# Front products of a decoder layer in 512 weight columns a matmul instead of 256

## The chip, the core and the metric

One core of a Trainium2 chip runs the whole layer. The engines in what follows are PE (TensorE, the matmuls), PEld (its weight loads), DVE (VectorE), ACT (ScalarE), POOL (GpSimd) and SP (SyncE, whose queue starts most of the transfers). The metric is device time in microseconds (us) for one execution, the median of several.

## What is computed

A decoder layer on 256 tokens of 1024 features, float32 throughout:

```python
h = layer_norm(DEEPNORM_ALPHA * h + hybrid_mixer(h, ...))        # DSA heads and GLA heads, then w_out
h = layer_norm(DEEPNORM_ALPHA * h + memory_cross_attention(h, mem, w_q, w_k, w_v, w_o))
h = layer_norm(DEEPNORM_ALPHA * h + peer(h, ...))                # product keys, 16 experts a head of 16384
# in hybrid_mixer: proj = x @ w_in, split in q, k, v, q_idx, k_idx, w_idx, g_q, g_k, g_v, g_lr, g_r
#   DSA: index scores pick 64 keys a query, softmax attention over those; GLA: gated linear attention
#   y = concat(y_dsa, y_gla) @ w_out
# in memory_cross_attention: k = mem @ w_k, v = mem @ w_v
```

The products that the change touches are `x @ w_in` for q, k, v, g_v and g_r, the mixer's output `y @ w_out`, and the first 512 of the 1024 columns of `mem @ w_v`.

## The kernel before

A float32 product is made of three float32r products: each operand is split in a rounded part and a remainder (`whi`, `wlo` for a weight; `xPh`, `xPl` for the input, likewise `yP`, `mP`, `hP`), and hi·hi, hi·lo and lo·hi are summed in PSUM.

Weights come in tiles of 1 MB, `w`, from a ring of three buffers; `wget` (L115) issues the transfer on SP's queue. `split` (L233) takes half a tile: ACT writes `whi` (L237), then DVE writes `wlo` (L239). Both lie in a ring `gd` of five buffers, so at most two and a half pairs exist at once, and a new `whi` or `wlo` waits until PE has finished with a pair. A half tile is 24 matmuls of 256 columns.

`proj` (L252) multiplies for both blocks of 128 tokens with the token block stationary and the weights moving. Its weight tile holds all 1024 rows of 256 columns; the two tiles of a 512-column result (`w1a`, `w1b` and so on) fill the two halves of one PSUM bank. `projT` (L268) does the transposed products (g_q, g_k, memory keys, queries) with the weights stationary and 256 token columns moving.

The front of the program is a set of generators, played in an order written out by hand: `FRONT` (L51) has a letter a step, `p` for the input products (q, k, gqk, v, gr, gv in that order), `a` and `b` for index selection and sparse attention of the two token blocks, `g` for linear attention, `m` for the memory keys and values. Then `MID` (L53) plays the mixer output (`mixed`, L828) against the rest of `m`. A scheduler then sets each engine's order from its own estimate of durations, so the order on an engine can differ from the text. Each engine works through its own order without overtaking.

The front's DVE work beside `wlo` is chiefly the index selection: `sc` (L394, L396) sums scores, and eight rounds of MAX (L402) and MATCH_REPLACE (L403) find the 64 largest. After the mixer output come layer norm 1 (L186 to L196), the queries (`mm<-hP`), memory attention, layer norm 2, and the expert part: row gathers on POOL (L899), the dense products `sc<-h2T,d` fed by transfers, and 1536 products `py` at the end.

Of the kernel before, what the change touches and what calls it, by code (L numbers as in the profile page):

```python
# [13 lines left out]
FT = mybir.dt.float32  # L14
# [4 lines left out]
AF = mybir.ActivationFunctionType  # L19
# [64 lines left out]
def kernel(ctx: ExitStack, tc, I, out):  # L84
    nc = tc.nc
    vec, act, gp = nc.vector, nc.scalar, nc.gpsimd
    pe = Counted(nc.tensor)
# [5 lines left out]
    wpool = ctxL.enter_context(tc.tile_pool(name="wpool", bufs=3))  # L93
# [6 lines left out]
    def mmt(name="mm"):  # L100
        return pmm.tile([128, 512], FT, tag="mm", name=name)
# [14 lines left out]
    def wget(nm):  # L116

        if nm in first:
            return first.pop(nm)
        src = I[nm]  # L120
        t = wpool.tile([128, 8, 256], FT, tag="w", name="w")
        nc.sync.dma_start(out=t[:, :, :src.shape[2]], in_=src)
        return t


# [5 lines left out]
    for i in range(4):  # L131
        k, cs = i // 2, slice(2 * (i % 2), 2 * (i % 2) + 2)
# [6 lines left out]
    ii = load(consts, "ii", [128, 2, 128])  # L139
    ident, iot = ii[:, 0, :], ii[:, 1, :]  # L140
    first["w1a"] = wget("w1a")
    gup = load(pers, "gup", [16, 256])
    gmask = load(pers, "gmask", [128, 128], I32)
# [6 lines left out]
    xv = pers.tile([128, 2, DM], FT, name="xv")  # L150
# [82 lines left out]
    def split(src, n, c=4):  # L233

        hi = gath.tile([128, c, n], FR, tag="gd", name="whi")
        lo = gath.tile([128, c, n], FR, tag="gd", name="wlo")
        act.activation(hi, src, AF.Copy)  # L237
        eng = gp if POOL[next(turn) % len(POOL)] else vec
        eng.tensor_sub(lo, src, hi.bitcast(FT))  # L239
        return hi, lo  # L240

    def pair(name):
        return [[slot(name + h, [128, 4, S], FR) for k in range(2)] for h in "hl"]

    def split_to(x, k, src, at=slice(None)):
        act.activation(x[0][k][at], src, AF.Copy)  # L246
        vec.tensor_sub(x[1][k][at], src, x[0][k][at].bitcast(FT))

    def parts(a, b):
        return ((a[0], b[0]), (a[0], b[1]), (a[1], b[0]))  # L250

    def proj(xP, nms, ps):  # L252

        o = 0
        for nm in nms:
            w = wget(nm)
            n = I[nm].shape[2]
            for k in range(2):
                wp = split(w[:, 4 * k:4 * k + 4, :n], n)
                for b in range(2):  # L260
                    for c in range(4):
                        for m, (l, r) in enumerate(parts([x[k] for x in xP], wp)):
                            pe.matmul(ps[b][:, o:o + n], lhsT=l[:, c, b * 128:(b + 1) * 128], rhs=r[:, c, :],
                                      start=(k == 0 and c == 0 and m == 0), stop=(k == 1 and c == 3 and m == 2))
                    yield
            o += n

    def projT(nm, xP, ps):  # L268

        w = wget(nm)  # L270
        for k in range(2):
            wp = split(w[:, 4 * k:4 * k + 4, :], 256)
            yield from products_T(wp[0], wp[1], xP, ps, k)
# [54 lines left out]
    def proj_in(nms, name, n):  # L328
        ps = [mmt() for _ in B2]
        yield from proj(xP, nms, ps)  # L330
        for b in B2:
            t = V[b][name]
            act.activation(t, ps[b][:, :n] if len(t.shape) == 2 else
                           ps[b][:, :n].rearrange("p (h d) -> p h d", d=t.shape[2]), AF.Copy)
# [237 lines left out]
    def memory_keys():  # L572
        memT = wget("memT")
        mP = pair("mP")
        for k in range(2):
            split_to(mP, k, memT[:, 4 * k:4 * k + 4])
        for i in range(4):
            ps = [mmt(), mmt()]
            yield from projT("xk%d" % i, mP, ps)
            for e in range(2):  # L580
                act.activation(xkT[:, 2 * i + e, :], ps[e][:, 0:256], AF.Copy)
        done.add("xk")
        for i in range(4):
            ps = [mmt(), mmt()]
            yield from proj(mP, ["xv%d" % i], ps)
            for m in range(2):
                act.activation(xv[:, m, i * 256:(i + 1) * 256], ps[m][:, 0:256], AF.Copy)

    def residual(b, xT_, nm, src, dst):

# [176 lines left out]
    xP = pair("xP")  # L767
# [45 lines left out]
    def play(streams, score):  # L813

        for ch in score:
            next(streams[ch], None)

    mk = memory_keys()
    front = dict(a=itertools.chain(index_select(0), sparse_attention(0)),
                 b=itertools.chain(index_select(1), sparse_attention(1)),  # L820
# [10 lines left out]
    def mixed():  # L831
        for i in range(2):
            nc.sync.dma_start(out=gb[:, i], in_=bcast_row(I["lnr"][i:i + 1, :], DM))
        for i in range(2):
            ps = [mmt() for _ in B2]
            yield from proj(yP, ["wo%d" % (2 * i), "wo%d" % (2 * i + 1)], ps)
            cs = slice(i * 512, (i + 1) * 512)
            for b in B2:
                vec.scalar_tensor_tensor(r1[b][:, cs], xb[b][:, cs], ALPHA, ps[b], op0=OP.mult, op1=OP.add)
        for b in B2:  # L840
            layer_norm(r1[b], (gb[:, 0], gb[:, 1]), h1[b], small)
# [219 lines left out]
    for now in range(128):  # L1061
        for i, span in enumerate(PICKS):
            if now >= span[0]:
                if i not in gpick:
                    begin(i)
                n = 18 if todo[i][2] == 2 else 12
# [10 lines left out]
        if now == CHANGE:  # L1077
            ctxP.close()
            wp = ctxB.enter_context(tc.tile_pool(name="wp", bufs=2))
# [100 lines left out]
    for b in B2:  # L1180
# [5 lines left out]
        if b == 0:  # L1186
# [4 lines left out]
            cs = slice(FB, DM)  # L1191
# [8 lines left out]
    cs = slice(0, FB)  # L1200
# [6 lines left out]
def _chunk(w, cols):  # L1207

    return np.ascontiguousarray(w[:, cols].reshape(8, 128, -1).transpose(1, 0, 2))
# [55 lines left out]
```

## Time and profile before

| what | before |
|---|---|
| median of 3 runs | 1048.31 us (1044.84 to 1048.84) |
| the profiled execution, device time | 1042.45 us |
| its span, first to last instruction | 1040.7 us |
| PE busy | 937.0 us (90%), 6650 matmuls |
| PEld busy | 870.2 us (84%) |
| DVE busy | 826.9 us (79%) |
| ACT busy | 420.2 us (40%) |
| POOL busy | 386.9 us (37%) |
| mean granted clock of PE | 0.966 of 2.4 GHz |

Shares over the whole span hide that the stages differ. A matmul's busy time overlaps the next one's, so what a product costs is read from start to start of a run of them, not from its own duration. Where an engine stands idle, the view says what released it; where it is not idle, its order alone sets the time.

### The profile page before, as it was taken

The numbers are of one execution on the slowest core, as the hardware profiler recorded it, in microseconds if no ns is written. First come the engines' busy times: TensorE is split into PE (matmuls) and PEld (weight loads), VectorE is DVE, ScalarE is ACT, GpSimd is POOL, SyncE is SP. The second block draws the span as 40 slices with busy tenths as digits, with TensorE's granted clock in tenths as the row PEclk, the third lists the DMA queues.
The fourth block names the chain that finished last, engine by engine and source line by source line (L and its number), as shares of the span: only waits on it lengthen the run. The fifth ranks groups of instructions, "written<-read, shape, count | busy, mean of one in ns | idle before, by whom it ended". The sixth has DMA issues, their size and how long they took to land.

```text
span 1040.7 us, 17837 instructions
## 1 busy us (share of the span) xinstructions
PE 937.0 (90%) x6650; PEld 870.2 (84%) x6650; DVE 826.9 (79%) x1944; ACT 420.2 (40%) x686; POOL 386.9 (37%) x263
## 2 busy tenths in 40 slices
PE   6999999897866977988699989899999999999994
PEld 6998879897756977887599989899888888888883
DVE  5967866745797998996699975855888988889896
ACT  5548664353211232322022231322655555655561
POOL 0000000000447454334545510000577777777772
PEclk9999999898998989999899989999999999999997
DMA  8555233445699989999989989264799999999992
GB/s 291 187 168 197 82 123 127 163 161 198 240 340 322 374 283 409 384 403 400 367 302 369 403 319 326 97 218 161 273 324 316 324 320 319 317 321 317 326 316 72
DMA packets 73974, 285.13 MB, mean 274 GB/s; under 512 B 9488, under 2 KB 10016, under 8 KB 67872
## 3 DMA queue, kind: packets, MB, share of 16 engines
q1 hardware_dynamic: 46976, 190.66, 51.5%
q0 software_dynamic: 26624, 92.29, 24.0%
q8 instruction: 52, 0.85, 0.3%
q10 hardware_dynamic: 288, 1.05, 0.3%
q14 instruction: 34, 0.28, 0.1%
HBM read 282.91 MB, written 1.05 MB: 273 GB/s over the span
## 4 chain that ended last, share of the span: by engine, by line
PE 62%; DVE 14%; DMA 14%; issue 4%; ACT 3%; POOL 1%; SPq 0%; ACTq 0%; POOLq 0%; DVEq 0%
PE py L76 28%; PE mm L76 17%; PE sc L76 10%; DMA d<-dnT 9%; DMA gd<-dn,ei 4%; DVE gd L901 4%; DVE oa L1008 3%; PE wb L76 3%; DVE o L1003 2%; POOL gd L899 1%; PE tp L80 1%; DVE wlo L239 1%; DMA w<-xo 1%; PE go L76 1%; ACT whi L237 1%
## 5 line engine op out<-in xcount | busy, mean ns | idle before, releaser
L899 POOL DMA_INDIRECT gd<-dn,ei x128 | 160.6, 1255 | 430.9 <-ACT s1b L877 268.3
L934 POOL DMA_INDIRECT gu<-upg,ei x128 | 221.6, 1731 | 203.2 <-DVE yq L1120 133.5
L76 PE MATMUL sc<-h2T,d 128*128 128x128 f32 x2048 | 255.0, 280 | 25.9 <-DMA d<-dnT 24.6
L76 PEld LDWEIGHTS sc<-h2T,d 128*128 128x128 f32 x2048 | 242.6, 195 | 32.9 <-DMA d<-dnT 16.2
L76 PE MATMUL py<-uh,w 128*128 128x320 f32 (+1 forms) x1024 | 235.5, 352 | 1.0 <-ACT uh L1153 1.0
L76 PEld LDWEIGHTS py<-uh,w 128*128 128x128 f32 x1024 | 177.4, 189 | 22.9 <-ACT uh L1153 1.2
L1153 ACT ACTIVATE uh<-u 128x1024 fp32r<-128x1024 f32 x128 | 135.7, 1062 | 116.9 <-PE py L76 77.6
L1154 DVE TENSOR_TENSOR ul<-u,uh 128x1024 fp32r<-128x1024 f32 x128 | 156.5, 1224 | 31.0 <-issue 16.1
L901 DVE CUSTOM_DVE_ANT_0 gd<-gd,h 128x1024 f32<-128x1024 f32 x128 | 155.2, 1224 | 23.8 <-DMA gd<-dn,ei 23.7
L76 PE MATMUL py<-ul,w 128*128 128x320 f32 (+1 forms) x512 | 138.9, 352 | 0.7 <-DVE ul L1154 0.7
L239 DVE TENSOR_TENSOR wlo<-w,whi 128x1024 fp32r<-128x1024 f32 (+1 forms) x68 | 81.3, 1197 | 47.5 <-PE mm L76 35.7
L76 PEld LDWEIGHTS py<-ul,w 128*128 128x128 f32 x512 | 91.1, 189 | 12.5 <-DVE ul L1154 1.0
L237 ACT ACTIVATE whi<-w 128x1024 fp32r<-128x1024 f32 (+1 forms) x68 | 70.4, 1038 | 54.1 <-PE mm L76 40.1
L1008 DVE TENSOR_SCALAR oa<-ii,ixT,wT 128x128 f32<-128x128 f32 x256 | 72.5, 359 | 23.3 <-PE wb L76 22.5
L76 PE MATMUL wb<-oa,o 128*128 128x128 f32 x512 | 75.1, 287 | 13.3 <-DVE oa L1008 13.2
L1012 ACT ACTIVATE W<-wb 128x512 f32<-128x512 f32 x64 | 38.2, 596 | 117.6 <-PE wb L76 114.1
L76 PEld LDWEIGHTS wb<-oa,o 128*128 128x128 f32 x512 | 66.7, 196 | 16.0 <-DVE oa L1008 9.2
L1122 DVE SCALAR_TENSOR_TENSOR yq<-gu,wt,yq 128x384 f32<-128x384 f32 x127 | 78.0, 614 | 0.1
L76 PE MATMUL mm<-h2T,w 128*128 128x128 f32 x448 | 54.9, 283 | 3.4 <-DMA w<-pq 3.4
L76 PEld LDWEIGHTS mm<-h2T,w 128*128 128x128 f32 x448 | 53.7, 200 | 4.1 <-DMA w<-pq 4.1
L76 PE MATMUL mm<-whi,xPh 128*128 128x256 f32 (+1 forms) x176 | 50.9, 292 | 6.6 <-ACT xPh L246 6.6
L76 PE MATMUL mm<-wlo,xPh 128*128 128x256 f32 (+1 forms) x176 | 52.0, 296 | 1.6 <-DVE wlo L239 1.6
(327 smaller groups left out, 1369.7 us busy)
## 6 DMA issues: line engine op xcount, KB each, us to landing
d<-dnT SPq DMA_DIRECT2D x128, 512.0 KB
u<-upd SPq DMA_DIRECT2D x128, 512.0 KB
w<-pq SPq DMA_DIRECT2D x10, 1024.0 KB
w<-xo SPq DMA_DIRECT2D x8, 1024.0 KB
w<-xk SPq DMA_DIRECT2D x4, 1024.0 KB
w<-xv SPq DMA_DIRECT2D x4, 1024.0 KB
w<-wo SPq DMA_DIRECT2D x4, 1024.0 KB
w<-xq SPq DMA_DIRECT2D x4, 1024.0 KB
```

The costliest lines, as they stand in the source:

```text
L76: self.eng.matmul(out, lhsT=lhsT, rhs=rhs, **kw)
L237: act.activation(hi, src, AF.Copy)
L239: eng.tensor_sub(lo, src, hi.bitcast(FT))
L899: gp.indirect_dma_start(out=g, out_offset=None, in_=I["dn"], in_offset=bass.IndirectOffsetOnAxis(ap=ei[:, k:k + 1], axis=0))
L901: vec.tensor_tensor_reduce(out=g, in0=g, in1=H2[0], scale=1.0, scalar=0.0, op0=OP.mult, op1=OP.add, accum_out=wt[:, k:k + 1])
L934: gp.indirect_dma_start(out=g, out_offset=None, in_=I["upg"], in_offset=bass.IndirectOffsetOnAxis(ap=PK[b]["ei"][:, k:k + 1], axis=0))
L1003: vec.tensor_tensor(o2, iot[:, None, :].to_broadcast([128, 8, 128]), ix2[:, 4 * g:4 * g + 8, None].to_broadcast([128, 8, 128]), op=OP.is_e ...
L1008: vec.tensor_scalar(a, iot, ixT[:, t:t + 1], wT[:, t:t + 1], op0=OP.is_equal, op1=OP.mult)
L1012: act.activation(W[0][:, :, 4 * g - 4:4 * g], ps[g - 1].rearrange("p (j i) -> p i j", j=4), AF.Copy)
L1122: vec.scalar_tensor_tensor(y, g, wt[:, k:k + 1], y, op0=OP.mult, op1=OP.add)
L1153: act.activation(uh, u, AF.Copy)
L1154: vec.tensor_sub(ul, u, uh.bitcast(FT))
```

## The change

The weights of q, k, v, g_v, g_r, of the mixer output and of the first half of the memory values are laid out so that a 1 MB tile holds 512 rows of 512 columns instead of 1024 rows of 256. `proj` now runs over two such tiles; a half tile is two chunks of 128 rows by 512 columns, still 1024 elements a partition for ACT and DVE, and 12 matmuls of 512 columns instead of 24 of 256. A matmul writes a whole PSUM bank. `proj_256` is the old form, kept for the last two memory value tiles, which come later. The number of steps a tile is played in stays four. Bytes, transfers and splits stay as many as before.

```diff
 def wget(nm):
-        t = wpool.tile([128, 8, 256], FT, tag="w", name="w")
-        nc.sync.dma_start(out=t[:, :, :src.shape[2]], in_=src)
+        t = wpool.tile([128, src.shape[1], src.shape[2]], FT, tag="w", name="w")
+        nc.sync.dma_start(out=t, in_=src)
...
     def proj(xP, nms, ps):
-        o = 0
-        for nm in nms:
+        for k, nm in enumerate(nms):
             w = wget(nm)
             n = I[nm].shape[2]
-            for k in range(2):
-                wp = split(w[:, 4 * k:4 * k + 4, :n], n)
+            for h in range(2):
+                wp = split(w[:, 2 * h:2 * h + 2, :], n, 2)
                 for b in range(2):
-                    for c in range(4):
-                        for m, (l, r) in enumerate(parts([x[k] for x in xP], wp)):
-                            pe.matmul(ps[b][:, o:o + n], lhsT=l[:, c, b * 128:(b + 1) * 128], rhs=r[:, c, :],
-                                      start=(k == 0 and c == 0 and m == 0), stop=(k == 1 and c == 3 and m == 2))
+                    for c in range(2):
+                        xs = [x[k][:, 2 * h + c, b * 128:(b + 1) * 128] for x in xP]
+                        for m, (l, r) in enumerate(parts(xs, wp)):
+                            pe.matmul(ps[b][:, 0:n], lhsT=l, rhs=r[:, c, :], start=(k == 0 and h == 0 and c == 0 and m == 0),
+                                      stop=(k == 1 and h == 1 and c == 1 and m == 2))
                     yield
-            o += n
...
-        for i in range(4):
+        for o, n in ((0, 512), (512, 256), (768, 256)):
             ps = [mmt(), mmt()]
-            yield from proj(mP, ["xv%d" % i], ps)
+            yield from proj(mP, ["xv0", "xv1"], ps) if n == 512 else proj_256(mP, "xv%d" % (o // 256), ps)
             for m in range(2):
-                act.activation(xv[:, m, i * 256:(i + 1) * 256], ps[m][:, 0:256], AF.Copy)
+                act.activation(xv[:, m, o:o + n], ps[m][:, 0:n], AF.Copy)
```

PE's order has 384 rows fewer than before, one for each pair of matmuls that became one. Lines from `projT` on move by 11 (L394 is L405). Beyond that the scheduler moves a few instructions of the front. On DVE, at the first index scores (`sc`; `wlo` here is the second half of the second q tile), before:

```order
L374 COPY glr<-tp 16x128
L394 TENSOR_SCALAR sc<-rl,wi 128x256
L396 SCALAR_TENSOR_TENSOR sc<-rl,wi,sc 128x256 x5
L239 TENSOR_TENSOR wlo<-w,whi 128x1024
L396 SCALAR_TENSOR_TENSOR sc<-rl,wi,sc 128x256 x2
L399 TENSOR_TENSOR sc<-sc,cst 128x128
```

and now:

```order
L385 COPY glr<-tp 16x128
L239 TENSOR_TENSOR wlo<-w,whi 128x1024
L405 TENSOR_SCALAR sc<-rl,wi 128x256
L407 SCALAR_TENSOR_TENSOR sc<-rl,wi,sc 128x256 x7
L410 TENSOR_TENSOR sc<-sc,cst 128x128
```

The remainder moved from the middle of the scores to ahead of them.

On ACT, in the first linear attention (`gl`, its gates) and where the memory keys begin (`whi` is the first half of their first tile), before:

```order
L475 ACTIVATE gl<-gl 128x256
L485 ACT_TABLE_LOAD
L485 ACTIVATE gl<-gl 128x256
L486 ACTIVATE gl<-gl 128x256
L237 ACTIVATE whi<-w 128x1024
```

and now:

```order
L486 ACTIVATE gl<-gl 128x256
L237 ACTIVATE whi<-w 128x1024
L496 ACT_TABLE_LOAD
L496 ACTIVATE gl<-gl 128x256
L497 ACTIVATE gl<-gl 128x256
```

The rounded part went ahead of the table load and two gate functions.

On PE, where the mixer output (`yP`) follows the memory values (`mP`) and the last transposes of linear attention (`yg`) stand, before:

```order
L76 MATMUL mm<-whi,mPl 128x256
L80 MATMUL tp<-ii,yg 128x128 x4
L76 MATMUL mm<-whi,mPh 128x256
L76 MATMUL mm<-wlo,mPh 128x256
L76 MATMUL mm<-whi,mPl 128x256
L76 MATMUL mm<-whi,yPh 128x256
```

and now:

```order
L76 MATMUL mm<-whi,yPh 128x512
L76 MATMUL mm<-wlo,yPh 128x512
L76 MATMUL mm<-whi,yPl 128x512
L76 MATMUL mm<-whi,yPh 128x512
L76 MATMUL mm<-wlo,yPh 128x512
L80 MATMUL tp<-ii,yg 128x128 x4
L76 MATMUL mm<-whi,yPl 128x512
```

The transposes moved from ahead of the last three memory products to behind the eighth matmul of the mixer output.

## Rows read from the trace of the kernel before

**Rows 1.** Busy time by stretch: length, PE, PEld, DVE, ACT, POOL; clock, DMA share, GB/s.
```profile
33.00:61.00 28.00, 27.77 (x234) 27.07 (x235) 27.05 (x81) 13.99 (x21) 0.00 (x0) 1.00 0.48 166
61.00:81.00 20.00, 20.00 (x168) 19.87 (x167) 8.85 (x10) 9.49 (x11) 0.00 (x0) 1.00 0.61 211
81.00:99.00 18.00, 16.86 (x139) 16.30 (x139) 14.81 (x21) 15.98 (x28) 0.00 (x0) 1.00 0.38 138
137.00:161.00 24.00, 23.05 (x178) 18.06 (x177) 17.16 (x49) 14.63 (x40) 0.00 (x0) 1.00 0.23 88
161.00:183.00 22.00, 22.00 (x186) 22.00 (x184) 13.06 (x13) 9.24 (x10) 0.00 (x0) 1.00 0.48 167
183.00:198.00 15.00, 10.88 (x78) 10.30 (x76) 14.65 (x39) 5.52 (x8) 0.00 (x0) 0.82 0.49 179
273.00:500.00 227.00, 181.58 (x1365) 168.84 (x1366) 197.51 (x720) 53.01 (x125) 107.82 (x89) 0.95 0.96 363
```

**Rows 2.** The chain that ended last: start us, length us, what.
```profile
33.20 11.95 PE mm L76 x95
...
60.72 18.88 PE mm L76 x155
...
273.64 7.97 DMA gd<-dn,ei
```

**Rows 3.** PE's instructions in order: start us, duration us; input products, 33 starts apart.
```profile
62.02 0.28 PE L76 MATMUL mm<-whi,xPl 128*128 128x256 f32 x1
...
65.98 0.28 PE L76 MATMUL mm<-whi,xPl 128*128 128x256 f32 x1
```

**Rows 4.** The same view in the last stage, `py`: pairs of 512 and of 320 columns.
```profile
757.22 0.62 PE L76 MATMUL py<-ul,w 128*128 128x512 f32 x2
757.68 0.91 PE L76 MATMUL py<-uh,w 128*128 128x512 f32 x4
758.43 0.46 PE L76 MATMUL py<-ul,w 128*128 128x320 f32 x2
758.72 0.92 PE L76 MATMUL py<-uh,w 128*128 128x320 f32 x4
```

**Rows 5.** The same view: the scores' matmuls, first remainder products of four half tiles.
```profile
23.76 1.17 PE L76 MATMUL dots<-kiT,qiT 32*128 32x256 f32 x16
...
29.84 0.39 PE L76 MATMUL mm<-wlo,xPh 128*128 128x256 f32 x1 [0.90 <-DVE wlo L239]
...
33.20 0.39 PE L76 MATMUL mm<-wlo,xPh 128*128 128x256 f32 x1 [0.23 <-DVE wlo L239]
...
39.16 0.39 PE L76 MATMUL mm<-wlo,xPh 128*128 128x256 f32 x1
...
42.14 0.39 PE L76 MATMUL mm<-wlo,xPh 128*128 128x256 f32 x1
```

**Rows 6.** DVE's instructions in order, the index scores and first selection rounds.
```profile
25.55 0.35 DVE L394 TENSOR_SCALAR sc<-rl,wi 128x256 f32<-128x256 f32 x1 [2.28 <-ACT rl L389]
...
28.57 1.22 DVE L239 TENSOR_TENSOR wlo<-w,whi 128x1024 fp32r<-128x1024 f32 x1
29.71 1.00 DVE L396 SCALAR_TENSOR_TENSOR sc<-rl,wi,sc 128x256 f32<-128x256 f32 x2
...
31.93 1.22 DVE L239 TENSOR_TENSOR wlo<-w,whi 128x1024 fp32r<-128x1024 f32 x1
...
34.91 1.22 DVE L239 TENSOR_TENSOR wlo<-w,whi 128x1024 fp32r<-128x1024 f32 x1
```

**Rows 7.** PE and DVE in order, where the memory keys begin.
```profile
90.50 0.39 PE L76 MATMUL mm<-mPh,whi 128*128 128x256 f32 x1 [1.14 <-ACT whi L237]
...
89.32 1.22 DVE L239 TENSOR_TENSOR wlo<-w,whi 128x1024 fp32r<-128x1024 f32 x1
```

**Rows 8.** ACT and DVE in order: a split in the second linear attention, and `yg`.
```profile
141.51 1.04 ACT L237 ACTIVATE whi<-w 128x1024 fp32r<-128x1024 f32 x1
...
159.56 0.69 DVE L565 TENSOR_TENSOR yg<-yg,gr 128x512 f32<-128x512 f32 x1
```

More of the change, by code (lines that the diff above doesn't have):

```diff
@@ L252, in proj, with proj_256 @@
     def proj(xP, nms, ps):
-        o = 0
-        for nm in nms:
+        for k, nm in enumerate(nms):
             w = wget(nm)
             n = I[nm].shape[2]
-            for k in range(2):
-                wp = split(w[:, 4 * k:4 * k + 4, :n], n)
+            for h in range(2):
+                wp = split(w[:, 2 * h:2 * h + 2, :], n, 2)
                 for b in range(2):
-                    for c in range(4):
-                        for m, (l, r) in enumerate(parts([x[k] for x in xP], wp)):
-                            pe.matmul(ps[b][:, o:o + n], lhsT=l[:, c, b * 128:(b + 1) * 128], rhs=r[:, c, :],
-                                      start=(k == 0 and c == 0 and m == 0), stop=(k == 1 and c == 3 and m == 2))
-                    yield
-            o += n
+                    for c in range(2):
[3 more added lines that the diff above has]
+                                      stop=(k == 1 and h == 1 and c == 1 and m == 2))
+                    yield
+    def proj_256(xP, nm, ps):
+        w = wget(nm)
+        for k in range(2):
+            wp = split(w[:, 4 * k:4 * k + 4, :], 256)
+            for b in range(2):
+                for c in range(4):
+                    for m, (l, r) in enumerate(parts([x[k] for x in xP], wp)):
+                        pe.matmul(ps[b][:, 0:256], lhsT=l[:, c, b * 128:(b + 1) * 128], rhs=r[:, c, :],
+                                  start=(k == 0 and c == 0 and m == 0), stop=(k == 1 and c == 3 and m == 2))
+                yield
     def projT(nm, xP, ps):
@@ L1239 @@
     for i, c0 in ((1, 0), (2, 512), (3, 1024), (4, 1832), (5, 2872), (6, 2344)):
-        a["w%da" % i] = _chunk(win, R(c0, c0 + 256))
-        a["w%db" % i] = _chunk(win, R(c0 + 256, c0 + 512))
+        for h in range(2):
+            nm, cs = "w%d%s" % (i, "ab"[h]), slice(4 * h, 4 * h + 4)
+            if i == 4:
+                a[nm] = _chunk(win, R(c0 + 256 * h, c0 + 256 * h + 256))
+            else:
+                a[nm] = A(_chunk(win, R(c0, c0 + 512))[:, cs])
     for nm, w, n in (("wo", w_out, 4), ("xk", xattn_w_k, 4), ("xv", xattn_w_v, 4), ("xq", xattn_w_q, 4),
@@ L1245 @@
         for i in range(n):
-            a["%s%d" % (nm, i)] = _chunk(w, R(i * 256, (i + 1) * 256))
+            if nm == "wo" or nm == "xv" and i < 2:
+                a["%s%d" % (nm, i)] = A(_chunk(w, R(i // 2 * 512, i // 2 * 512 + 512))[:, i % 2 * 4:i % 2 * 4 + 4])
+            else:
+                a["%s%d" % (nm, i)] = _chunk(w, R(i * 256, (i + 1) * 256))
     a["gup"] = A(gla_gate_up)[0]
```

## The prediction

> **What bounds the kernel now.** The change touches only work that ends at about 183 us, so I read the front stage by stage and ask of each what ends last there. First the table by stretch [rows 1]: PE is busy 27.77 of 28 us, 20 of 20, 16.86 of 18, 23.05 of 24 and 22 of 22 in the stretches that hold changed products. By that alone the whole front would be PE's, and every matmul saved would count. The second view speaks against it: the chain that ended last [rows 2] gives PE 95 matmuls in 11.95 us from 33.20 (0.1258 us each) and 155 in 18.88 us from 60.72 (0.1218, with some records missing), but the bare run of the same matmul is 33 starts in 3.96 us, 0.1200 each [rows 3]. So something holds PE back between 33 and 45 us without showing as idle time.
>
> The third view says what. The first remainder products of half tiles start at 33.20, 39.16 (two half tiles on) and 42.14 us [rows 5]: every 2.98 us, where 24 matmuls of 0.1200 make 2.88. Each of these rows is drawn out to 0.39 us, where its neighbours take 0.28. DVE makes the remainders at 31.93 and 34.91 [rows 6], the same 2.98 us apart, with two selection rounds between them, and is busy 27.05 of 28 us from 33 to 61 [rows 1]. DVE's order, not PE, sets this stretch. From 61 on DVE has slack (8.85 of 20 us) and PE is the bound. From 81 to 99 ACT is nearly full (15.98 of 18) and PE waits 1.14 us once. From 161 to 183, the mixer output, PE is full again with DVE at 13.06 of 22.
>
> Behind 183 us nothing is edited. Layer norm 1 is DVE's (14.65 of 15 us, [rows 1]). The expert part starts when the front has chosen rows, with the gathers, whose rows are awaited from 273.64 us [rows 2],, and then keeps the DMA engines at a 0.96 share for 227 us. Its transfers wait for the front's results and buffers, so I take it to move with the front, one for one.
>
> **The change part by part.** *What a wide matmul costs.* No row before has 512 columns in the front, but `py` has them in the same type: two start 0.46 us apart from the next two, 0.230 each, and two of 320 columns take 0.29, 0.145 each [rows 4]. Two of 256 cost 0.240. So a pair saves 10 ns by the row. The other bound: at full clock (2.4 GHz) 256 columns take 106.7 ns, so 13.3 of the 120.0 ns are overhead, and if that is paid once instead of twice a pair saves 13.3. I take 10 as the direct reading. 384 pairs (5 input products of 48, the mixer output's 96, the memory values' 48) are then worth 3.84 us of PE time, at most 5.1.
>
> The Trainium skill (TensorE: Matmul & The Clock Gate, section Back-to-back issue gap) puts the isolated spacing at N/2.4 + 2.5 ns; by that a pair would save only 2.5 ns, an estimate of 1.0 us in all. It also gives about 131 ns as the sustained spacing at 512 columns, by which a pair would save 109 ns and the front about 42 us, again an estimate. The trace agrees with neither: 120.0 ns at 256 and 230 ns at 512 columns.
>
> *0 to 61 us* (q, k, and the start of v, 4 tiles of q and k). PE's own saving here would be 96 × 10 ns = 0.96 us and a bit of v, but DVE sets the pace. What counts is whether DVE's order starts sooner. Before, it stands idle 2.28 us until 25.55, does six score steps, one remainder (28.57 to 29.71, 1.14 us) and two more scores [rows 6]. Now that remainder comes first. It needs a buffer that PE frees with the first q tile. The scores' own matmuls stand in PE's order just before the last matmul of that tile, which before run from 23.76 to 24.93 [rows 5]; now the columns of five narrow matmuls more (0.6 us) stand ahead of them, less what the others save, and one wide matmul behind them ends the tile; I put the buffer at 25.25 (an estimate, between 24.9 and 25.8). From there the same instructions follow without a gap, so DVE is 25.55 − 25.25 = 0.3 us ahead of before (−0.25 to +0.65). PE's stall of 0.90 us at 29.84 [rows 5] goes, but it is only moved: the remainder at 31.93 would come at about 31.6, and PE, ready sooner, waits for that. Term: **0.3 us**, from −0.3 to 0.7.
>
> *61 to 81 us* (v and g_r). Seven half tiles from 60.72 [rows 2] are PE-bound: 7 × 12 pairs × 10 ns = **0.84 us**, up to 1.12.
>
> *81 to 99 us* (g_v). Four half tiles hold 0.48 us. ACT is nearly full. Its reordered split would end PE's wait at 90.50, but DVE's remainder of 89.32, which the next product needs and which ends about 90.5, stays where it was [rows 7], so I expect most of the wait to stay, with DVE named instead of ACT. Term: **0.2 us**, from 0 to 0.64.
>
> *99 to 161 us* (memory keys unchanged; 48 pairs of the memory values). 0.48 us of PE work, in a stretch where PE idles 0.95 of 24 us and the attention chain runs through ACT and DVE. A split of 1.04 us [rows 8] now stands ahead of the last gate functions on ACT and can delay them by its length. Term: **0.25 us**, from −1.05 to 0.64.
>
> *161 to 183 us* (mixer output). 96 pairs × 10 ns = **0.96 us**, up to 1.28. The transposes `yg` now stand behind eight wide matmuls (1.84 us), but DVE has a remainder of 1.14 us and the product `yg` of 0.69 [rows 8] to do after the memory values free a buffer, 1.83 to 1.9 us: at most 0.1 us of waiting, or some 0.3 if that remainder starts late. Low end 0.6.
>
> *Rest.* Two evictions of 512 replace four of 256 on ACT, off the path. The three remainders inside layer norm 1 stay three. Transfers are as many and as large, the ring is the same, and SP only swaps one weight tile with two loads of `x` that nothing needs before the mixer output. Cost 0, hidden behind some 140 us of other work; were that cover gone, the loads would stand in the mixer output's eviction.
>
> Sum: 0.3 + 0.84 + 0.2 + 0.25 + 0.96 = **2.55 us** gained, between 0.1 and 4.4. Against the profiled execution (1042.45 us, of which 1040.7 are its span) that is 1039.9. It lies 5.9 us below the median, so I carry the difference and not the level: 1048.31 − 2.55 = **1045.8 us**.
>
> **Rivals.** *DVE and ACT take it all.* If the stretches to 161 us give nothing and the DMA-bound stage does not start sooner by the rest, only part of the mixer output's 0.96 counts: 1047.8 us. For: DVE at 27.05 of 28, DMA at 0.96. Against: 20 of 20 us PE-bound from 61. *Everything counts, and the waits go too.* 5.1 us of matmuls plus PE's 1.14 us wait [rows 7] is 6.2: 1042.1 us. For: PE's busy shares. Against: the 2.98 us beat. *A wide matmul is far cheaper than `py` shows*, because consecutive ones overlap when nothing else holds PE: with a spacing near that of one 256-column matmul (0.12 us, [rows 3]), the 84 + 96 pairs of the two PE-bound stretches alone would save 21.6 us: 1026.7 us. The row at 0.230 speaks against it. The skill's 131 ns, named above, would be this case. *Slower: the ring of five buffers.* Three splits now stand at the head of an engine's order, ahead of an attention chain (the three places shown), and one more ahead of the last gate functions. Each waits for PE to free a pair. If the pair comes half a tile (2.76 us) late at three of them, the chains behind start later by 8.3 us, less the PE-bound 1.8: +6.5, 1054.8 us. It decides from the moment at which ACT or DVE gets there before PE has left the tile ahead. At 81 to 99 us PE is the one that waits for ACT, so it is ahead, against it; at the scores the two nearly coincide.
>
> **How the numbers follow.** Forecast 0.64, the all-taken case 0.14, everything counts 0.13, far cheaper 0.01, slower 0.08. A measurement of this kernel can tell about 0.5% (5.2 us) from no change, and the runs before spread over 4 us. The forecast's own bounds are 1043.9 to 1048.2; with 2 us each way for the median of a few runs, and reaching to the everything case, the range is 1041 to 1050. Faster by over 0.5% (below 1043.1): 0.14 from the two fast cases and 0.04 from the forecast's edge, 0.18. Slower by over 0.5%: 0.07, most of the slow case. Within: 0.75.
>
> **What would show it.** Right: matmuls of 512 columns 0.230 us apart from 62 us on; first remainder products still 2.98 us apart between 33 and 43 us, with more waiting for `wlo` than before; the mixer output in about 22.1 us instead of 23.0; layer norm 1 starting 2 to 3 us earlier and every later stage with it. Wrong: the beat at 33 to 43 gone (then more is gained), ACT or DVE idle until PE frees a buffer at the moved splits (then less), or a later stage, the DMA-bound one above all, ending when it did before although it started sooner.

## The result, and the profile after

The changed kernel was measured twice, each time beside the kernel before on the same chip. The first time it took 1042.76 us (median of 12 runs, 1038.2 to 1047.88) against 1049.8 us: ratio 0.9942, 95% interval 0.9922 to 0.9963. The second time it took 1044.74 us against 1048.48 us: ratio 0.9953, 0.9934 to 0.9973. The ratio is estimated from all the runs and is not the quotient of the two medians, which differ by 7.0 and 3.7 us. By the ratio 6.1 and 4.9 us were gained where 2.55 were forecast. The time lies inside the range of 1041 to 1050 us, but the gain is twice the forecast's and above the 4.4 us at which the bounds of its sum end; it stands at the edge between "within 0.5%" and "faster". The profiled execution took 1043.47 us (span 1041.7). That of the kernel before (1042.45) lay below all twelve runs of the kernel before that stood beside the changed one, so the two spans can't be subtracted. Stages can.

The first view is the table by stretch, for the changed kernel (columns as in [rows 1]):

```profile
33.00:61.00 28.00, 27.83 (x177) 23.53 (x176) 27.21 (x79) 13.24 (x19) 0.00 (x0) 1.00 0.47 154
61.00:81.00 20.00, 20.00 (x90) 16.28 (x89) 10.15 (x12) 11.26 (x13) 0.00 (x0) 1.00 0.55 208
81.00:99.00 18.00, 17.49 (x103) 14.54 (x101) 15.04 (x24) 15.90 (x30) 0.00 (x0) 1.00 0.50 198
137.00:161.00 24.00, 23.57 (x137) 15.71 (x136) 15.91 (x46) 13.76 (x36) 0.00 (x0) 1.00 0.31 115
161.00:183.00 22.00, 22.00 (x115) 18.92 (x115) 15.70 (x24) 8.50 (x8) 0.00 (x0) 1.00 0.50 165
183.00:198.00 15.00, 10.19 (x60) 9.24 (x59) 11.21 (x31) 4.48 (x8) 0.00 (x0) 0.77 0.53 197
273.00:500.00 227.00, 178.59 (x1321) 166.16 (x1320) 191.09 (x704) 51.54 (x121) 98.53 (x85) 0.92 0.94 353
```

Beside [rows 1] almost nothing seems to have happened: PE is as full as it was, in stretches of the same clock time. The difference is in what it does in them. PE's chain of the input products, 18.88 us from 60.72 before [rows 2], is now

```profile
59.39 17.76 PE mm L76 x77
```

and starts 1.33 us earlier. PE's instructions in order (start us, duration us) give the price of a wide matmul, in the mixer output:

```profile
159.00 0.40 PE L76 MATMUL mm<-whi,yPh 128*128 128x512 f32 x1
...
177.82 0.39 PE L76 MATMUL mm<-whi,yPl 128*128 128x512 f32 x1
```

There are 84 of them in a row from the first to the last shown, so 83 intervals in 18.82 us: 0.2267 us each, where two narrow ones took 0.2400 [rows 3]. A pair saves 13.3 ns, the upper bound of the prediction. 0.2267 is 512 columns at 2.4 GHz (0.2133) plus the same 13.3 ns that a narrow one pays on its 0.1067.

The beat at 33 to 43 us stayed. First remainder products of half tiles:

```profile
32.12 0.50 PE L76 MATMUL mm<-wlo,xPh 128*128 128x512 f32 x1 [1.22 <-DVE wlo L239]
...
35.10 0.50 PE L76 MATMUL mm<-wlo,xPh 128*128 128x512 f32 x1
...
38.08 0.50 PE L76 MATMUL mm<-wlo,xPh 128*128 128x512 f32 x1
...
41.05 0.50 PE L76 MATMUL mm<-wlo,xPh 128*128 128x512 f32 x1
```

They stand 2.98 us apart as in [rows 5], though twelve wide matmuls need only 2.72; the row that follows each wait is drawn out. But the whole beat starts earlier. DVE's order at the scores, changed kernel:

```profile
23.79 1.23 DVE L239 TENSOR_TENSOR wlo<-w,whi 128x1024 fp32r<-128x1024 f32 x1 [1.01 <-PE mm L76]
25.41 0.35 DVE L405 TENSOR_SCALAR sc<-rl,wi 128x256 f32<-128x256 f32 x1 [0.39 <-ACT rl L400]
25.80 3.83 DVE L407 SCALAR_TENSOR_TENSOR sc<-rl,wi,sc 128x256 f32<-128x256 f32 x7
...
30.85 1.22 DVE L239 TENSOR_TENSOR wlo<-w,whi 128x1024 fp32r<-128x1024 f32 x1
...
33.82 1.22 DVE L239 TENSOR_TENSOR wlo<-w,whi 128x1024 fp32r<-128x1024 f32 x1
```

The remainder lies in the gap in which DVE had stood idle for 2.28 us [rows 6]; the scores start at 25.41 instead of 25.55, and the next remainders at 30.85 and 33.82 instead of 31.93 and 34.91.

To compare stages between executions I count time from the first remainder of a full half tile (17.20 us before, 16.89 after), since the first weights arrive up to a microsecond sooner or later from run to run, and I take as the end of the front the first transposes of layer norm 1's result. The row before is

```profile
194.49 3.84 PE L80 MATMUL tp<-ii,h 128*128 128x128 f32 x16 [4.12 <-DVE h L196]
```

and the row after

```profile
188.73 1.35 PE L80 MATMUL tp<-ii,h 128*128 128x128 f32 x8 [4.09 <-DVE h L196]
```

So the front ends at 177.29 before and 171.84 after: **5.45 us** earlier (5.42 in the second profile of the changed kernel). By stage, with the forecast beside it:

| stretch | forecast (range) | measured | from |
|---|---|---|---|
| 0 to 61 us | 0.3 (−0.3 to 0.7) | 1.02 | start of the PE-bound chain, 60.72 and 59.39, less the 0.31 of the start-up |
| 61 to 81 | 0.84 (to 1.12) | 1.12 | its length, 18.88 and 17.76 |
| 81 to 99 | 0.2 (0 to 0.64) | 0.83 | first masked attention logits, 99.16 and 95.88, less the stages ahead |
| 99 to 161 | 0.25 (−1.05 to 0.64) | 1.24 | what is left |
| 161 to 183, mixer output | 0.96 (0.6 to 1.28) | 1.24 | mixer output alone, below |
| sum | 2.55 (0.1 to 4.4) | 5.45 | |

### The profile page after: what moved, and what is told of

Its sections match the earlier page's. It is cut to its first block, busy times and chain, and to the rows that moved or that the text cites. A ratio compares the mean times of both kernels' runs of the same rounds, so it can differ in the third digit from the quotient of the medians.

```text
span 1041.7 us, 17060 instructions
## 1 busy us (share of the span) xinstructions
PE 934.3 (90%) x6266; PEld 849.0 (82%) x6266; DVE 826.4 (79%) x1944; ACT 420.2 (40%) x684; POOL 378.6 (36%) x263
## 3 DMA queue, kind: packets, MB, share of 16 engines
q10 hardware_dynamic: 288, 1.05, 0.3%
HBM read 282.91 MB, written 1.05 MB: 273 GB/s over the span
## 4 chain that ended last, share of the span: by engine, by line
PE 68%; DMA 14%; DVE 11%; ACT 3%; issue 3%; POOL 1%; SPq 0%; ACTq 0%; DVEq 0%; POOLq 0%
PE py L76 28%; PE mm L76 16%; PE sc L76 15%; DMA d<-dnT 9%; PE wb L76 5%; DMA gd<-dn,ei 4%; DVE wlo L239 2%; DVE gd L912 1%; PE tp L80 1%; DVE oa L1019 1%; POOL gd L910 1%; PE go L76 1%; DMA w<-xo 1%; DVE o L1014 1%; DVE sc L414 1%
## 5 line engine op out<-in xcount | busy, mean ns | idle before, releaser
L910 POOL DMA_INDIRECT gd<-dn,ei x128 | 153.7, 1201 | 441.6 <-ACT s1b L888 263.0
L1159 DVE TENSOR_TENSOR w<-W,w 128x512 fp32r<-128x512 f32 x64 | 41.2, 685 | 3.6 <-ACT w L1158 3.6
L936 ACT ACTIVATE W<-sc 128x512 f32<-128x512 f32 x20 | 12.0, 598 | 79.6 <-PE sc L76 79.6
```

The lines of the kernel that those rows point to most:

```text
L910: gp.indirect_dma_start(out=g, out_offset=None, in_=I["dn"], in_offset=bass.IndirectOffsetOnAxis(ap=ei[:, k:k + 1], axis=0))
L1159: vec.tensor_sub(w[:, 1], src, w[:, 0].bitcast(FT))
```

## The experiments

Front is the change of the point just named against the kernel before (negative is earlier). The time is a ratio to runs of the kernel before in the same job, with its 95% interval.

| kernel | front, us | ratio |
|---|---|---|
| whole change | −5.45, −5.42 | 0.9942 (0.9922 to 0.9963), 0.9953 (0.9934 to 0.9973) |
| input products alone | −3.42 | 0.9981 (0.9958 to 1.0004) |
| mixer output alone | −1.24 | 1.0001 (0.9975 to 1.0027) |
| memory values alone | −0.68 | 0.9997 (0.9977 to 1.0018) |
| tiles without wide matmuls | +0.95 | 1.001 (0.9984 to 1.0037) |
| before, remainder ahead of the scores | −0.89 | 1.0001 (0.9983 to 1.002) |
| changed, remainder back among the scores | −4.53 | none; a single execution of 1048.83 us |
| changed, four remainders on GpSimd | +0.96 | 1.0019 (0.9994 to 1.0044) |
| changed, one selection later | −5.20 | 0.9942 (0.992 to 0.9964) |
| changed, mixer output without its third term | −9.79 | 0.9911 (0.9882 to 0.9939) |
| changed, third term twice | +1.64 | 1.0065 (1.0041 to 1.0089) |

**Parts: which products give the gain?** Each kernel keeps the old `proj` (here `proj_old`) and the old tiles for the rest. Input products alone:

```diff
-            yield from proj(yP, ["wo%d" % (2 * i), "wo%d" % (2 * i + 1)], ps)
+            yield from proj_old(yP, ["wo%d" % (2 * i), "wo%d" % (2 * i + 1)], ps)
...
-        for o, n in ((0, 512), (512, 256), (768, 256)):
+        for o, n in ((0, 256), (256, 256), (512, 256), (768, 256)):
```

> Wide matmuls for the five input products alone (240 pairs); mixer output and memory values stay at 256 columns. Theory that each part gives its own share and that all of it reaches the end: the first eviction of the mixer output, at 183.21 us before and 177.57 with the whole change, comes near 179.5, the 61 us point and the 81 to 99 stretch as with the whole change (chain of 17.8 us from 59.4, no PE wait for a rounded part near 90), and the run is about 3.7 us faster than before (ratio 0.9965). Rival, the parts hang together (the mixer output's share comes only because the front is ahead of it): the eviction comes near 183 minus 1 to 2 us, and the ratio is 0.998 or above.

Mixer output alone (`proj_old` in `proj_in`, memory values in four parts):

```diff
     def proj_in(nms, name, n):
-        yield from proj(xP, nms, ps)
+        yield from proj_old(xP, nms, ps)
```

> Wide matmuls for the mixer output alone (96 pairs). Theory, each pair saves the 13.3 ns of the front's own rows (0.2270 us at 512 columns against 0.1200 at 256): the stretch to 161 us stays as before and the first eviction of the mixer output comes 1.3 us earlier than 183.21, near 181.9; ratio near 0.9988, which this measurement can hardly tell from 1. With the 10 ns of the prediction it would be 0.96 us, near 182.25. Rival, a wide matmul that streams better between long runs of its own kind: 2 us or more.

Memory values alone (`proj_old` for both of the others):

> Wide matmuls for the first half of the memory values alone (48 pairs). Theory, 13.3 ns a pair: 0.64 us at layer norm 1, whose first transposes come near 176.6 us after the fifth weight remainder is counted as 0 at 17.20 before (177.29 before), ratio 0.999 to 1. Rival, PE is not the bound of that stretch and the rounded part that moved ahead of the gate functions costs: 0 to 1 us later than before.

Measured at the end of the front: 3.42, 1.24 and 0.68 us, together 5.34 of the whole's 5.45. The parts add, and two of them lie where 13.3 ns a pair puts them: 96 pairs are 1.28 us, 48 pairs 0.64. The rival of parts that hang together falls. Of the delay by the rounded part ahead of the gate functions nothing is left at the end of the front; it did show on the way there (99 to 161 us, below). In the total none of the three can be told from no change; their changes sum to 2.2 us, with some 2.5 us of uncertainty each, which is too coarse to add up. The front's landmark repeated within 0.1 us, where the ratio of twelve runs resolves 2.

**Width or tiles?** The changed kernel with two matmuls of 256 columns for each wide one, all else as changed:

```diff
-                            pe.matmul(ps[b][:, 0:n], lhsT=l, rhs=r[:, c, :], start=(k == 0 and h == 0 and c == 0 and m == 0),
-                                      stop=(k == 1 and h == 1 and c == 1 and m == 2))
+                            for js in (slice(0, 256), slice(256, 512)):
+                                pe.matmul(ps[b][:, js], lhsT=l, rhs=r[:, c, js], start=(k == 0 and h == 0 and c == 0 and m == 0 and js.start == 0),
+                                          stop=(k == 1 and h == 1 and c == 1 and m == 2 and js.start == 256))
```

> The new weight tiles (512 rows by 512 columns) and the new order of steps everywhere, but each matmul issued as two of 256 columns, so that the count of matmuls is that of before. Theory, the width makes the gain beyond 61 us: the chain from 61 to 81 us is as long as before (18.9 us for seven half tiles), the mixer output too, the 61 us point stays at 60.7, and the run is within 1 us of before (ratio 0.999 to 1.001). Rival, the tile layout and the order that comes with it make the gain: ratio near that of the whole change (0.994).

The front ends 0.95 us later than before and the total is the same (1.001). At the end of the front nothing of a gain comes from the tiles and their order alone; the rival falls. On the way part of a gain does: where PE waits 1.14 us before [rows 7], it waits 0.32 here, with narrow matmuls,

```profile
88.66 0.51 PE L76 MATMUL mm<-wlo,xPh 128*128 128x256 f32 x2 [0.32 <-DVE wlo L239]
```

so that shorter wait, which the changed kernel has as well, comes with the order and not with the width. It is lost again in two waits for remainders that the kernel before does not have (0.99 us at 121.79, 0.62 at 137.01). With narrow matmuls the scheduler keeps the remainder among the scores, so this kernel lacks the moved remainder too.

**0 to 61 us: width, or the moved remainder?** Two kernels, one for each half of the question. First the kernel before with all its narrow matmuls, and the first score pinned behind the remainder (the next remainder behind the last score, so that it doesn't slip in as well):

```diff
-FRONT = ('bppppppppppppppppabpppppappbg...
+FRONT = ('pppppppbpppppppppabpppppappbg...
...
-        eng.tensor_sub(lo, src, hi.bitcast(FT))
+        with tc.issue_after(scored[0]) if len(rem) == 8 else ExitStack():
+            rem.append(eng.tensor_sub(lo, src, hi.bitcast(FT)).ins)
...
+                        with tc.issue_after(rem[7]) if b else ExitStack():
+                            vec.tensor_scalar(sc[:, :nk], rl[:, j, :nk], wi[:, 0:1], None, op0=OP.mult)
```

> The kernel before with matmuls of 256 columns throughout; only DVE's order is moved by hand: the remainder that stood in the middle of the first index scores goes ahead of them, into the 2.28 us in which DVE stood idle, with PE's order around the scores' matmuls left as it was. Theory, the 1.33 us gained by 61 us come from this filled slot and not from wide matmuls: DVE's selection rounds start about 1.1 us earlier (first round at 31.07 before), and the PE-bound stretch starts near 59.6 instead of 60.72; ratio near 0.999. Rival, the gain comes from the wide matmuls: the stretch starts near 60.7 as before, and PE waits longer for its own work.

Second the changed kernel with that remainder put back behind six scores:

```diff
-        eng.tensor_sub(lo, src, hi.bitcast(FT))
+        with tc.issue_after(scored[5]) if next(nth) == 7 else ExitStack():
+            eng.tensor_sub(lo, src, hi.bitcast(FT))
```

> The changed kernel with DVE's order of the kernel before at one place: the remainder goes back into the middle of the first index scores, behind six of them. Theory, most of the gain by 61 us is the idle slot of DVE that this remainder filled: the PE-bound stretch starts about 1 us later than 59.39, and layer norm 1 too. Rival, the wide matmuls made it: it starts at 59.4 to 59.6.

The order is worth 0.89 us at the end of the front with narrow matmuls and 5.45 − 4.53 = 0.92 us with wide ones. So of the 1.02 us by 61 us about 0.9 come from the order, and the width itself adds 0.1 there. It is the worth of an order and not of one instruction: in both kernels the scheduler also set later remainders among the selection rounds. The mechanism that I had named for it, the filled gap, holds only for wide matmuls. In the first of the two kernels DVE's row is

```profile
25.03 1.23 DVE L241 TENSOR_TENSOR wlo<-w,whi 128x1024 fp32r<-128x1024 f32 x1 [2.66 <-PE mm L76]
```

and PE's

```profile
22.64 0.28 PE L76 MATMUL mm<-wlo,xPh 128*128 128x256 f32 x1
22.85 1.17 PE L76 MATMUL dots<-kiT,qiT 32*128 32x256 f32 x16
...
24.28 0.28 PE L76 MATMUL mm<-wlo,xPh 128*128 128x256 f32 x1
...
24.64 0.28 PE L76 MATMUL mm<-wlo,xPh 128*128 128x256 f32 x1
```

The gap stayed open for 2.66 us, until the last `wlo` product of the tile (24.64), which with narrow matmuls stands behind the scores' own. There the gain came differently: remainders went ahead of selection rounds, and PE did not wait once between 17.6 and 88.7 us, where the kernel before waits 0.90 and 0.23 [rows 5]. With wide matmuls the same place in PE's order reads

```profile
23.29 0.39 PE L76 MATMUL mm<-wlo,xPh 128*128 128x512 f32 x1
23.61 1.17 PE L76 MATMUL dots<-kiT,qiT 32*128 32x256 f32 x16
24.71 0.50 PE L76 MATMUL mm<-whi,xPl 128*128 128x512 f32 x1
```

The last `wlo` product is ahead of the scores' matmuls; only a product of `whi` is left behind them. The buffer of the remainder is free at about 23.7 us, and DVE takes it at 23.79. In the second kernel PE paid for the old order twice, 1.52 and 0.69 us:

```profile
29.24 0.50 PE L76 MATMUL mm<-wlo,xPh 128*128 128x512 f32 x1 [1.52 <-DVE wlo L240]
...
50.48 0.39 PE L76 MATMUL mm<-xPh,wlo 128*128 128x256 f32 x1 [0.69 <-DVE wlo L240]
```

**Can DVE be relieved, and does it beat the change?** Two tries, both on the changed kernel. Four of the remainders on GpSimd, which has nothing to do there (the tuple has a 1 at the splits 9, 11, 14 and 16):

```diff
-POOL = (0,)
+POOL = (0, 0, 0, 0, 0, 0, 0, 0, 0, 1, 0, 1, 0, 0, 1, 0, 1, ...)
```

> The changed kernel with four of the remainders between 33 and 55 us (every second one) made on GpSimd instead of DVE; PE's and ACT's orders are the same. Theory, DVE's order sets the pace from 31 to 59 us: freed of four times 1.14 us, DVE stops being late there, half tiles follow each other in 2.72 us (12 wide matmuls of 0.2267) instead of 2.98, and the PE-bound stretch starts 1 to 2.5 us earlier than at 59.39; ratio 0.992 to 0.993. Rival, the remainder on GpSimd takes about 2.9 us (1.99 us for 704 columns in the last stage, scaled to 1024, an estimate), later than PE needs it: PE waits for it in four places and the stretch starts at 59.4 or later; ratio 0.994 or above.

The front ends 6.4 us later than with the changed kernel, and the ratio is 1.0019: the rival's side, though not for the rival's reason alone. PE waits twice for more than 3 us, the first time at

```profile
34.15 0.50 PE L76 MATMUL mm<-wlo,xPh 128*128 128x512 f32 x1 [3.18 <-DVE wlo L239]
```

and the two engines' rows show why:

```profile
30.66 2.35 POOL L239 TENSOR_TENSOR wlo<-w,whi 128x1024 fp32r<-128x1024 f32 x1 [29.40 <-ACT qk L344]
...
30.92 3.18 DVE L239 TENSOR_TENSOR wlo<-w,whi 128x1024 fp32r<-128x1024 f32 x1
```

GpSimd's remainder takes 2.35 us, until 33.01. DVE's own, issued 0.26 us later, takes 3.18 instead of 1.22 and ends at 34.10, 1.09 us behind GpSimd's end: it stood still until GpSimd was through. The second remainder on GpSimd ran beside selection rounds, and those kept their length:

```profile
39.71 2.57 POOL L239 TENSOR_TENSOR wlo<-w,whi 128x1024 fp32r<-128x1024 f32 x1 [6.70 <-PE mm L76]
...
39.94 0.42 DVE L413 MAX8 m<-sc 128x8 f32<-128x256 f32 x1
```

The Trainium skill (SBUF — State Buffer, section SBUF: two separate sides) says that GpSimd shares a port pair with VectorE's instructions that read two operands from SBUF, as an exclusive lock for the whole instruction. Both pairs of rows agree with it, and my expectation had left the lock out.

The other try plays the scores and selection of the first token block two half tiles later:

```diff
-FRONT = ('bppppppppppppppppabpppppappbgppbpaapppmppp...
+FRONT = ('bppppppppppppppppbppppaaaapppbgppbppppmppp...
```

> The changed kernel with the index scores and selection of the first token block played four steps (two half tiles) later, so that DVE's 16 instructions of scores and rounds after 45 us fall where PE has more ahead of it; PE's order changes only in those eight small matmuls. Theory, DVE sets the pace until 59 us and has slack behind: the half tiles after 45 us follow in 2.7 to 2.9 us instead of 2.98 to 3.17, the stretch in which PE never waits starts sooner, and layer norm 1 comes 1 to 2.5 us earlier than with the changed kernel; ratio to before 0.992 to 0.9945. Rival, the lock is only moved to the later place, or the sparse attention that follows comes late: layer norm 1 at the same time or later.

The front ends 0.25 us later than with the changed kernel; the total (0.9942) can't be told from it. DVE's rows show the first half of the rival:

```profile
46.45 1.22 DVE L239 TENSOR_TENSOR wlo<-w,whi 128x1024 fp32r<-128x1024 f32 x1
49.21 1.23 DVE L239 TENSOR_TENSOR wlo<-w,whi 128x1024 fp32r<-128x1024 f32 x1 [0.81 <-PE mm L76]
...
51.21 2.88 DVE L407 SCALAR_TENSOR_TENSOR sc<-rl,wi,sc 128x128 f32<-128x128 f32 x7
54.34 1.22 DVE L239 TENSOR_TENSOR wlo<-w,whi 128x1024 fp32r<-128x1024 f32 x1
```

The half tiles come at 2.76 us while the scores are away and DVE even idles for a buffer, then 5.13 us pass around the scores: five buffers don't hold more of the lead. And there was little to win: PE is busy 18.00 of 18 us from 43 to 61 here, and 17.83 with the changed kernel, whose first remainder products are drawn out by 0.1 us at 33 to 43 us and hardly at all between 45 and 59. DVE sets the pace from 31 to 43 us, and after that only once more, for 0.17 us at 59.39. So no version tried beats the change clearly.

**Does the end move with the front?** The mixer output with 32 wide matmuls fewer and 32 more, 7.25 us each way. The first leaves out the product of the rounded weight with the input's remainder; the second adds that product twice:

```diff
-            yield from proj(yP, ["wo%d" % (2 * i), "wo%d" % (2 * i + 1)], ps)
+            yield from proj(yP, ["wo%d" % (2 * i), "wo%d" % (2 * i + 1)], ps, 2)
...
-                        for m, (l, r) in enumerate(parts(xs, wp)):
+                        for m, (l, r) in enumerate(parts(xs, wp)[:terms]):
```

> The changed kernel without the third term (rounded weight times remainder of the input) of the mixer output: 32 wide matmuls less, which at 0.2267 us each are 7.25 us less in the stretch from 159 to 178 us, where PE is the bound. Theory, later stages move one for one with the front: layer norm 1 comes 7 us earlier than with the changed kernel (somewhat less if splits or weight transfers fall behind), and the run is 7 us faster than that: ratio to the kernel before 0.9942 minus 0.007, near 0.987. Rival, the DMA-bound expert part ends when it did before: ratio near 0.994, the 7 us turning into longer waits behind 265 us.

> The changed kernel with the third term of the mixer output added twice: 32 wide matmuls more, 7.25 us more in the same stretch. Theory, one for one: ratio to the kernel before near 1.001. Rival, the expert part absorbs what the front does: ratio near 0.994.

The front moved by 11.43 us between the two (the shorter one gains only 4.3 of its 7.25: PE then waits for remainders at 165.73 and 174.98, 0.56 and 1.04 us; the rest I did not trace), and the end by 0.0154 of 1048.6, 16.1 us. An expert part that absorbs the front's gain would show the same end for both; that rival falls. The longer kernel ends later than one for one would have it (6.8 us, interval 4.3 to 9.3, for 1.64 at the front). Single executions take 846 to 858 us from the end of the front to the end of the run whatever the kernel. The longer kernel's trace has its extra time in the part of the experts: from DVE's first work on a gathered row to the last product `sc<-h2T` it takes 470.1 us, the other traces 457 to 468. Why is open.

The changed kernel once more, beside those:

> The changed kernel itself once more, beside the next two on one chip. Layer norm 1 comes 5.4 us earlier than before, the input products alone brought 3.4, the mixer output alone 1.2, and the doses of 14.5 us more and less moved the end by 16.1. Theory, one for one: 4.5 to 6.5 us faster than before, ratio 0.994 to 0.9955. Rival, the 6.1 us of the first measurement held some luck and later stages keep a part: ratio 0.996 to 0.9985, which would also suit the parts (0.9981 and 1.0001).

Ratio 0.9953: 4.9 us (2.8 to 6.9) for 5.42 at the front. The first theory's 0.994 to 0.9955 contains it. The rival's 0.996 to 0.9985 overlaps the upper third of this interval, and of the first measurement's (to 0.9963) only the edge; a small loss behind the front is not excluded.

## Why the prediction came out as it did

The order of the reading was right, and the structure of the sum too: stage by stage, later stages one for one within the 2 us that the runs resolve (the kernel with the third term twice stands out). The sign held, and the time lies in the range. The size was off by a factor of two: 5.45 us at the front are more than the 4.4 at which the sum's bounds end, and three of its five terms came out above their own. The range took the time in because it had been widened for the median and towards a rival. The causes:

- **What a pair saves.** 13.3 ns, not 10. I took the `py` row over the other bound. That row is read at 10 ns on two matmuls, so the pair's 10 ns carried an uncertainty as large as the difference between the bounds. The bound from overhead paid once was the better one, and 83 intervals in the changed kernel confirm it. It puts 384 pairs at 5.1 us instead of 3.84. The mixer output (0.96 forecast, 1.24 measured) and 61 to 81 us (0.84, 1.12) are off by this alone. A longer run was in the trace of before: ten rounds of `py` from 750.44 to 773.04 us, each of six matmuls of 512 columns and six of 320, take 2.26 us each, which leaves 15.0 ns beside the columns and 11.7 for a pair, between the bounds.
- **0 to 61 us.** 0.3 was forecast and 1.02 came. That DVE's order decides there was right (0.9 of the 1.02 is order). The buffer was mis-dated: 25.25 us by my estimate, 23.79 in the row. I had taken the tile's last matmul, behind the scores' own, as what frees it. What frees a remainder's buffer is the last product that reads a remainder, and that one stands ahead of the scores' matmuls when matmuls are wide. That DVE sets the pace up to 61 us was too far: from 43 on PE is the bound, but for the 0.17 us at 59.39.
- **81 to 99 us.** I expected most of PE's 1.14 us wait to stay, with DVE named. The waits were read rightly. Once ACT no longer holds PE up, the next thing that PE needs is the remainder of 89.32 [rows 7], for `mm<-wlo,xPh` (at 90.72 us before, the product behind the one that waits), and DVE is named. But only for a third of the time:

```profile
87.27 0.50 PE L76 MATMUL mm<-wlo,xPh 128*128 128x512 f32 x1 [0.37 <-DVE wlo L239]
```

 ACT's row before was

```profile
89.41 1.04 ACT L237 ACTIVATE whi<-w 128x1024 fp32r<-128x1024 f32 x1
```

 In the changed kernel ACT writes the first rounded part of the memory keys ahead of the table load, and the wait for it is gone:

```profile
84.52 1.06 ACT L237 ACTIVATE whi<-w 128x1024 fp32r<-128x1024 f32 x1
85.59 1.28 ACT L496 ACT_TABLE_LOAD   x1
```

 The step that failed is that DVE's remainder stays where it was. DVE's order moved here too, which the list of moved instructions leaves out. Before, the last of four reciprocals of a gate (`sg`) stood between DVE's wait for `gl` and the remainder:

```profile
86.92 0.43 DVE L476 SCALAR_TENSOR_TENSOR gl<-gl 128x256 f32<-128x256 f32 x1 [1.22 <-ACT gl L475]
87.26 0.95 DVE L492 RECIPROCAL sg<-sg 128x128 f32<-128x128 f32 x1
```

 Now all four come ahead of that wait (80.48 to 83.87 us):

```profile
84.47 0.42 DVE L487 SCALAR_TENSOR_TENSOR gl<-gl 128x256 f32<-128x256 f32 x1 [0.61 <-ACT gl L486]
...
86.02 1.20 DVE L239 TENSOR_TENSOR wlo<-w,whi 128x1024 fp32r<-128x1024 f32 x1
```

 The remainder starts 1.55 us behind `gl` instead of 2.40, and 0.77 us of PE's wait are gone. The tiles without wide matmuls have this order and the short wait; the mixer output alone and the memory values alone have the old order and wait 1.14. With the stretch's 48 pairs (0.64 us by 13.3 ns) that makes 1.41. The table's 0.83 is read on DVE, where not all of it shows yet. On PE's own chain the first products `go` of linear attention start, before,

```profile
113.63 2.91 PE go L76 x24
```

 and now

```profile
109.86 2.91 PE go L76 x24
```

 which is 3.46 us earlier, counted as above: 1.32 more than the two stretches ahead.

- **99 to 161 us.** 0.25 forecast, 1.24 measured, of which some 0.5 belong to the stretch ahead: the input products alone are 2.94 us ahead at 95.80, and 3.42 both at the first `go` and at the end of the front. The rest is chiefly the memory values' 48 pairs, 0.68 (0.64 by 13.3 ns). The delay by the rounded part ahead of the last gate functions, which set the lower end, came and went. Those functions start at 140.55 before and 137.73 now, 2.51 us ahead where `go` had been 3.46; the second `go` (149.48 and 145.97) is 3.20 ahead; at the end of the front nothing of it is left. What made it up was not tested.
- **Carried as forecast:** the beat of 2.98 us with PE waiting a little longer for `wlo` (1.22 us against 0.90 and 0.23), later stages one for one, and level against difference (the profiled execution of before lay below its median, as noted).

Added up from these numbers, about 3.8 us of the 5.45 are the width (0.1 by 61 us, 1.12, 0.64, 0.64, 1.28) and about 1.7 the scheduler's new order (0.92 and 0.77). The 0.64 of 81 to 99 us is priced at 13.3 ns and not measured apart.

Of the rivals, "everything counts, and the waits go too" came nearest: 6.2 us, 1042.1, against 5.45 at the front and 4.9 to 6.1 at the end. I gave it 0.13 because the beat spoke against it. It is near partly by luck: the beat was real, the 96 pairs of q and k gave 0.1 us instead of 1.3, and the moved remainder made up for them. "Slower: the ring of five buffers" did not happen: after the moved splits no chain was late by the end of the front.

## What to carry to other kernels

Where two bounds for the price of an operation differ by less than the row can resolve, take the mechanism (columns at the clock plus a fixed part) or a longer run of the same instruction, and keep both in the sum. When an instruction is moved ahead of a wait, find the instruction that frees its buffer by what it reads, not by the end of the tile. When a scheduler sets the orders from its own durations, compare every engine's order over the whole changed stretch: about 1.7 of 5.45 us came from there. Judge small changes at a landmark behind the changed stage: it repeated within 0.1 us here, where twelve runs resolve 2. What reaches the end is a second question, and only the runs answer it.

## What the runs showed of the hardware

Matmuls of 256 and of 512 columns in float32r follow each other at 0.1200 and 0.2267 us where the granted clock is 1.00 (2.4 GHz): the columns' 0.1067 and 0.2133 and 13.3 ns, with nothing gained in a run of 84 of one kind. The Trainium skill (TensorE: Matmul & The Clock Gate, section Back-to-back issue gap) has 131 ns sustained at 512 columns and 215.8 ns (an estimate from its N/2.4 + 2.5) isolated; the trace agrees with neither. GpSimd and VectorE don't run subtractions of two operands side by side (3.18 us instead of 1.22), but selection rounds go on undisturbed (0.42). One of DVE's instructions with a single operand did not: a TENSOR_SCALAR of 128x256 at 41.91 us, beside GpSimd's remainder of 39.71, took 0.53 us instead of the 0.29 of the changed kernel.

A little of the gain is lent and returned behind the front. By stretch of 4 us, the changed kernel:

```profile
188.00:192.00 4.00, 2.55 (x14) 2.04 (x15) 3.86 (x10) 1.24 (x3) 0.00 (x0) 0.71 0.67 262
192.00:196.00 4.00, 4.00 (x20) 3.77 (x19) 1.97 (x4) 1.15 (x2) 0.00 (x0) 0.50 0.80 262
196.00:200.00 4.00, 4.00 (x33) 4.00 (x33) 1.23 (x1) 1.50 (x3) 0.00 (x0) 0.93 0.00 0
```

and the kernel before:

```profile
194.00:198.00 4.00, 3.51 (x16) 3.14 (x16) 3.90 (x9) 1.68 (x3) 0.00 (x0) 0.50 0.66 254
198.00:202.00 4.00, 4.00 (x29) 3.84 (x28) 1.54 (x4) 0.71 (x2) 0.00 (x0) 0.83 0.68 254
```

PE is thinly used in layer norm 1, and the granted clock falls to 0.50, the lower of its two levels (1.2 GHz). Before, most of that lies on the 16 transposes of layer norm 1's result (3.84 us); in the changed kernel it lies on the first 4 us of the queries, which take 24.84 us instead of 23.66 in the chain. At the end of the queries the lead is 4.07 us, counted as above. Most of the loss is made up later: DVE's first step on the experts' key scores, behind layer norm 2, starts 4.97 us earlier than before.

A fall of the clock to 0.50 also accounts for a part of the spread between executions. In five of the thirteen traces, that of the kernel before among them, it falls about 2 us after the first product `py`; these take 307.8 us from there to the end, the other eight 306.2.
